# A two-layer streaming encoder step on one core: where the conditioning pieces stand in a pair chunk's weight stream, and thirteen identity products at the start

## The chip, the cores and the metric

The kernel runs on one core of one Trainium2 chip. The metric is device time in microseconds (us), the median of several runs. TensorE (PE) multiplies matrices, VectorE (DVE) and ScalarE (ACT) work on elements, SyncE (SP) issues nearly all of the DMAs, GpSimd (POOL) does little here. "Clock" is the share of full speed that TensorE was granted, as the profile records it.

## What is computed

Two groups of rows, 1024 prompt rows and 32 sample rows of width 1024, go through two layers that share their weights. Cut to what matters:

```python
for i in range(2):
    mod = silu(c) @ w_ada[i] + b_ada[i]            # c: 1 x 1024, w_ada[i]: 1024 x 6144
    sh1, sc1, gt1, sh2, sc2, gt2 = split(mod, 6)
    h = rmsnorm(x, g[i, 0]) * (1 + sc1) + sh1
    mix = sgu_mixer(h) if i == 0 else pool_mixer(h)
    x = x + gt1 * rmsnorm(mix, g[i, 1])
    h = rmsnorm(x, g[i, 2]) * (1 + sc2) + sh2
    f = square(relu(h @ ffn_w_up[i])) @ ffn_w_down[i]   # 1024 -> 4096 -> 1024
    x = x + gt2 * rmsnorm(f, g[i, 3])
```

The six vectors of `mod` are the conditioning. Their matrix `w_ada` is 24 MB a layer, and each of the two `c` is one vector, so the conditioning is mostly loading. The first mixer starts with `v = gelu(h @ w_in)[:, 2048:]`.

## The kernel before

**Tiles.** The 1056 columns (rows of the reference, turned) are three tiles: 0 and 1 with 384 prompt columns each, 2 with 256 prompt and 32 sample columns. Each float32 operand is split in a high and a low part of the type fp32r (`split`, L1325; `w_split`, L498), and a product is three matmuls: high by high, high by low, low by high (`products`, L1061).

**The weight stream.** All weights come from HBM in one fixed order, the list `stream`. An entry is a 512 KB load; SP issues the loads in the order of the list into three raw buffers (`RAW_SLOTS`, L31; `issue`, L460). `stream_step` (L723) then consumes an entry: a weight is split by ACT (high part, L542) and DVE (low part) into one of 16 tiles (`do_w`, L534), and `need_w` gives it to PE. The raw buffer goes back when its last reader is done, and the next load can start.

**Conditioning pieces.** Among the weights stand pieces of `w_ada`. A late piece is 256 rows by 512 columns (`add_wide`, L297), and DVE multiplies it with the conditioning and adds it up in four instructions on 128 x 512 (`do_ada`, L614, tile `aa`). Every fourth piece ends with two transposes and two sums, and every second such end with small matmuls on PE (`fold`, L654). `some_ada(n)` puts the next n pieces of the list `rest` into the stream.

**Pair chunks.** In the feed-forward part, the list `passes` (L384) names for each layer seven pair chunks: 512 of the 4096 hidden columns each, for tiles 0 and 1 together. `w_chunk` (L352) writes a pair chunk's entries into the stream: four up weights, j = 0 to 3, in two groups of two, kinds `one` and `two`; then four down weights, q = 0 to 3. Its argument `ada` is the number of conditioning pieces that go between them: in layer 0 it is 5 for the first pair chunk, 6 for the next five and 1 for the last; in layer 1 it is 1 or 2 while pieces are left. A group of two up weights is turned by `quads` (L503), in four steps, into sums and differences of quarter matrices, A1, S31, S24 and A22, which need seven quarter products instead of eight (`pair_item`, L1569). PE's order in `up` (L1618) is: `pfa` from A1, `pfb` from S31, `pfa` from S24, `pfb` from S24, `pfa` from S31, `pfc` from A1, `pfa` from A22. Each product has twelve matmuls. Between the uses of an accumulator ACT copies it (`copy`, L1608, its line is L1610); PE may add to the accumulator only after that copy. `up(0)` and `up(1)` are followed by `down` (L1662), whose results DVE adds into `acc`.

**What sets the order.** Python code records the work with its own count of PE and DVE time (`time`, `weave`, L815), and the framework's scheduler then sets each engine's final order; the engines run that order strictly. The start, L1169 to L1242, is ordered by hand (`tc.manual_schedule()`) and stays as written.

**The start.** x arrives and is turned by PE (`x_turn`, L688). The first pieces of `w_ada` are multiplied on PE: four column blocks at a time (`do_ada_pe`, L578), then ACT copies the sum (`adas`, L595), and `fold` (L597) transposes it on PE with the identity `ident` and lets DVE finish a quarter of the scale (`sc1`, `sl` 4 to 7) or of the shift (`sh1`, `sl` 0 to 3). `first_norm` (L1038) makes `hh` (high, ACT) and `hl` (low, DVE) for two blocks of 128 rows of x at a time, and `early_mm` (L1125, matmuls at L1138) multiplies them with the first weight of the v half into `pv`: for three column blocks, twelve matmuls with the weight's high part and then six with its low part `wl_v`. The scratch accumulators of this stretch are a ring of three PSUM tiles (`ps_ms`, L143).

Of the kernel before, what the change touches and what calls it, by code (L numbers as in the profile page):

```python
# [15 lines left out]
P = 128  # L16
# [19 lines left out]
def tile_stream_encoder_step(  # L36
# [27 lines left out]
    mm = nc.tensor.matmul  # L64
# [47 lines left out]
    ident = const.tile([P, P], F32, name="ident")  # L112
# [24 lines left out]
    def ps_up(name):  # L137
        return psum.tile([P, 512], F32, tag="pu", bufs=2, name=name)
# [4 lines left out]
    def ps_ms(name):  # L143
        return psum.tile([P, 512], F32, tag="pm", bufs=3, name=name)
# [45 lines left out]
    def load_vectors(queue, i, part):  # L190
        at = sum(k for _, k in rows[i][: part.start])
        for ap, k in rows[i][part]:
            queue.dma_start(vec_rows[i][at : at + k, :P], ap)
            at += k
# [7 lines left out]
    def bring(func):  # L202

        act(out=junk1, in_=epsT, func=func)

    def turn_conditions():
        raw = vec_rows[2]
        act(out=raw[0:16, P : 2 * P], in_=raw[0:16, :P], func=AF.Silu)
        pt = ps_ms("csilT")
        nc.tensor.transpose(pt[:, 0:16], raw[0:16, P : 2 * P], ident[0:16, 0:16])  # L210
        nc.vector.tensor_copy(csil, pt[:, 0:16].rearrange("p (v k) -> p k v", v=NV))
        nc.vector.tensor_copy(csil32[:, :, 0:NV], csil)

    def turn_vectors():
        for raw, v in zip(vec_rows, vecs):
            n = v.shape[1]
            pt = ps_ms("rowT")
            nc.tensor.transpose(pt[:, :n], raw[:n, :P], ident[:n, :n])
            nc.vector.tensor_copy(v, pt[:, :n])
# [22 lines left out]
    def add_w(key, ap, shape, kind="w"):  # L242
        stream.append((kind, key, ap, shape))
# [108 lines left out]
    def w_chunk(n, ada=0):  # L352
        l, c, tiles, m = passes[n]
        left = [ada]

        def one_ada():
            if left[0] > 0:
                left[0] -= 1
                some_ada(1)

        for j in range(4 * m):
            f = 4 * c + j
            add_w(
                ("up", n, j),
                ffn_w_up[l][:, f * P : (f + 1) * P].rearrange("(k p) f -> p k f", p=P),
                (8, P),
                ("one", "two")[j % 2] if tiles == PAIR else "w",
            )
            if j % 2 == 1:
                one_ada()  # L370
        w = 256 // m
        for q in range(4 * m):
            add_w(
                ("dn", n, q),
                ffn_w_down[l][c * 512 : (c + m) * 512, q * w : (q + 1) * w].rearrange(
                    "(j p) d -> p j d", p=P
                ),
                (4 * m, w),
            )
            one_ada()  # L380

    every = list(range(NT))
    PAIR = every[:2]
# [10 lines left out]
    def some_ada(n):  # L394
        for _ in range(min(n, len(rest))):
            add, l, j = rest.pop(0)
            add(l, j)
# [62 lines left out]
    def issue():  # L460
        while state["issued"] < len(stream):
            k = state["issued"]
            kind, key, ap, shape = stream[k]
            if in_raw(k):
                if state["raw"] == RAW_SLOTS:
                    return
                state["raw"] += 1
                r = t_raw(f"raw{k}")
            elif kind == "x":
                r = x_rows[min(key // 3, NT - 1)]  # L470
                r = r[:, key % 3] if key < 6 else r
            else:
                r = w_tile(f"raw{k}")
            if kind == "x" and key < 6:
                i = nc.sync.dma_start(r, ap.rearrange("t (k n) -> t k n", n=P))
            elif kind == "x":
                for j in range(ap.shape[0] // 32):
                    for a in range(4):
                        i = nc.sync.dma_start(
                            r[32 * a : 32 * a + 32, 4 * (key - 6) + j],  # L480
                            ap[32 * j : 32 * j + 32].rearrange("s (k a m) -> s a k m", a=4, m=32)[:, a],
                        )
            else:
                i = nc.sync.dma_start(r.rearrange("p (a b) -> p a b", a=shape[0]), ap)
            raws[k] = r
            loads[key] = i.ins
            state["issued"] += 1
# [191 lines left out]
    def run_deferred(force=False):  # L679
        n = len(deferred)  # L680
        while n > 0 and (force or deferred[0][0] <= time["pe"]):
            deferred.pop(0)[1]()
            n -= 1
# [39 lines left out]
    def stream_step():  # L723

        if not subs and stream[state["next"]][0] == "one":
            issue()
            state["next"] += 1
        k = state["next"]
        kind, key, ap, shape = stream[k]
        issue()  # L730
        run_deferred()
        if kind == "two":
            if not subs:
                quads(key[1], key[2], raws.pop(k - 1), raws.pop(k))
            subs.popleft()[1]()
            if not subs:
                state["next"] += 1
            issue()
            return
        r = raws.pop(k)  # L740
        if kind == "w":
            do_w(key, r)
        elif kind == "wide":
            do_ada(*key, r, 512)
        elif kind == "ada":
            if k < first_ada:
                do_ada_pe(*key, r)
            else:
                do_ada(*key, r, 256)
        else:  # L750
            do_x(key, r)
        state["next"] += 1
        if in_raw(k):
            state["raw"] -= 1
        issue()
# [352 lines left out]
    def statistics(h):  # L1108
        while next(h) != "statistics":
            pass  # L1110

    def stream_to(kind, key):
        k = max(i for i, s in enumerate(stream) if s[0] == kind and s[1] == key)
        while state["next"] <= k:
            stream_step()
        run_deferred()
# [38 lines left out]
    def fold():  # L1155
        pe_folds.pop(0)()

    def turn():
        x_turns.popleft()()

    def lo():
        late_lo.popleft()()

    def row(h):

        next(h)
        next(h)

    with tc.manual_schedule():  # L1169
        load_vectors(nc.scalar, 2, slice(0, 2))  # L1170
        issue()
        load_vectors(nc.gpsimd, 0, slice(0, 1))
        load_vectors(nc.gpsimd, 1, slice(0, 1))
        load_vectors(nc.gpsimd, 2, slice(2, 4))
        bring(AF.Silu)
        stream_to("x", 0)
        turn_conditions()
        stream_to("x", 2)
        bring(AF.Sqrt)
        next(h0)  # L1180
        next(h0)
        stream_to("ada", (0, 4, 0))
        turn_vectors()
        stream_to("ada", (0, 4, 1))
        next(h0)
        statistics(h0)
        fold()
        next(h0)
        stream_to("ada", (0, 0, 1))
        fold()  # L1190
        stream_to("w", ("v", 0, 0))
        next(h0)
        late_hi.pop()()
        next(h0)
        lo()
        early_mm((0, 1, 2), 0)
        stream_to("x", 5)
        next(h1)
        turn()
        next(h1)  # L1200
        stream_to("ada", (0, 5, 1))
        turn()
        fold()
        next(h1)
        statistics(h1)
        turn()
        early_ps.extend(ps_up(f"pv0_{b}") for b in (3, 4))
        next(h1)
        row(h1)
        stream_to("ada", (0, 1, 1))  # L1210
        next(h0)
        early_mm((3,), 0)
        fold()
        early_mm((4,), 0)
        for q in range(1, 4):
            stream_to("w", ("v", 0, q))
            row(h0)
            lo()
            next(h1)
            row(h1)  # L1220
            if q == 3:
                stream_to("w", ("v", 1, 0))
            early_mm((0, 1), q)
            if q < 3:
                conditions(q + 1)
                fold()
                next(h0)
            early_mm((2,), q)
            if q < 3:
                fold()  # L1230
            early_mm((3, 4), q)
        bring(AF.Gelu_apprx_tanh)
        ps = ps_ms("pv0_5")
        v_mm(ps, 0, 5, range(KB))
        early_end((0,))
        stream_to("w", ("v", 1, 1))
        early_end((1, 2))
        stream_to("w", ("v", 1, 2))
        early_end((3,))
        stream_to("w", ("v", 1, 3))  # L1240
        early_end((4,))
        v_end(ps, 0, 5)  # L1242
# [40 lines left out]
    for p, b in v_order:  # L1283
        ps = ps_dn(f"pv{p}_{b}")
# [882 lines left out]
```

## Time and profile before

| | |
|---|---|
| median of 3 runs | 2106.61 us (2105.29 to 2107.28) |
| the profiled execution's own time | 2106.9 us |
| its span, first to last instruction | 2105.1 us |
| mean granted clock | 0.998 |
| POOL busy | 22.3 us |
| HBM read, written | 262.18 MB, 30.66 MB |
| mean HBM traffic over the span | 139 GB/s |

The profile is one execution. The 1.8 us between its time and its span lie before the first and after the last instruction. A group of instructions is named by its line, its engine and the tiles that it writes and reads, out<-in. A helper's line stands for all of its calls: L80 is every DVE operation of the kernel's own wrappers, and L1066 to L1068 are the three matmuls of a product. A busy PE is not a PE at its peak, since matmuls overlap, so the starts of matmuls in a row are read instead. PE loads weights on a path of its own (PEld, 96% busy).

### The profile page before, as it was taken

The numbers are of one execution on the slowest core, as the hardware profiler recorded it, in microseconds if no ns is written. First come the engines' busy times: TensorE is split into PE (matmuls) and PEld (weight loads), VectorE is DVE, ScalarE is ACT, GpSimd is POOL, SyncE is SP. The second block draws the span as 40 slices with busy tenths as digits, with TensorE's granted clock in tenths as the row PEclk, the third lists the DMA queues.
The fourth block names the chain that finished last, engine by engine and source line by source line (L and its number), as shares of the span: only waits on it lengthen the run. The fifth ranks groups of instructions, "written<-read, shape, count | busy, mean of one in ns | idle before, by whom it ended". The sixth has DMA issues, their size and how long they took to land.

```text
span 2105.1 us, 32717 instructions
## 1 busy us (share of the span) xinstructions
PE 2084.7 (99%) x12786; PEld 2013.1 (96%) x12786; DVE 1569.3 (75%) x2811; ACT 1034.3 (49%) x1853; POOL 22.3 (1%) x44
## 2 busy tenths in 40 slices
PE   8999999999999999999999999999999999999998
PEld 6878999999999999999999999999999999999998
DVE  6788737556869988888767989897868654579554
ACT  5634322234447644344446766776435443365555
POOL 0000000000000000000000000000000000001100
PEclk9999999999999999999999999999999999999999
DMA  8586524243524443443334667643223221148862
GB/s 295 159 268 213 187 79 135 85 150 106 159 70 156 130 126 113 128 126 115 114 96 130 207 198 238 192 140 106 92 76 109 88 80 52 54 125 233 202 180 93
DMA packets 397040, 294.98 MB, mean 140 GB/s; under 512 B 46638, under 2 KB 360278, under 8 KB 396884
## 3 DMA queue, kind: packets, MB, share of 16 engines
q1 hardware_dynamic: 395956, 291.60, 45.8%
q8 instruction: 100, 1.64, 0.3%
q0 software_dynamic: 896, 1.28, 0.2%
q14 instruction: 56, 0.46, 0.1%
q10 hardware_dynamic: 32, 0.01, 0.0%
HBM read 262.18 MB, written 30.66 MB: 139 GB/s over the span
## 4 chain that ended last, share of the span: by engine, by line
PE 89%; DVE 6%; ACT 2%; DMA 2%; issue 1%; SPq 0%; DVEq 0%; ACTq 0%
PE pg L1067 11%; PE pg L1066 11%; PE pg L1068 11%; PE pf L1066 4%; PE pf L1068 4%; PE pf L1067 4%; PE po L1066 3%; PE po L1067 3%; PE po L1068 3%; PE pfa L1604 3%; PE pfa L1606 3%; PE pfa L1605 3%; PE pu L1066 3%; PE pu L1068 3%; PE pu L1067 3%; PE pv L1092 2%
## 5 line engine op out<-in xcount | busy, mean ns | idle before, releaser
L1066 PE MATMUL pg<-fh,wh_dn 128*128 128x384 f32 (+1 forms) x960 | 311.2, 325 | 0.1
L1067 PE MATMUL pg<-fl,wh_dn 128*128 128x384 f32 (+1 forms) x960 | 310.8, 324 | 0.0
L1068 PE MATMUL pg<-fh,wl_dn 128*128 128x384 f32 (+1 forms) x960 | 310.0, 323 | 0.0
L80 DVE TENSOR_TENSOR acc<-acc,pg 128x384 f32<-128x384 f32 (+1 forms) x272 | 144.7, 533 | 111.9 <-PE pg L1068 110.7
L80 DVE TENSOR_TENSOR wl_dn<-raw,wh_dn 128x1024 fp32r<-128x1024 f32 x136 | 166.2, 1223 | 70.0 <-ACT wh_dn L542 36.7
L80 DVE SCALAR_TENSOR_TENSOR aa<-raw,csil,aa 128x512 f32<-128x512 f32 (+1 forms) x364 | 207.9, 621 | 13.0 <-DMA raw<-in_w_ada_dram 12.9
L1066 PE MATMUL pf<-hh,wh_up 128*128 128x288 f32 (+1 forms) x640 | 195.4, 305 | 0.4 <-ACT wh_up L542 0.4
L1067 PE MATMUL pf<-hl,wh_up 128*128 128x288 f32 (+1 forms) x640 | 194.0, 303 | 0.0
L1068 PE MATMUL pf<-hh,wl_up 128*128 128x288 f32 (+1 forms) x640 | 193.7, 303 | 0.0
L542 ACT ACTIVATE wh_dn<-raw 128x1024 fp32r<-128x1024 f32 x136 | 143.8, 1057 | 88.7 <-PE pf L1067 33.8
L1066 PEld LDWEIGHTS pg<-fh,wh_dn 128*128 128x128 f32 x960 | 180.2, 188 | 1.4 <-ACT fh L1326 1.0
L1067 PEld LDWEIGHTS pg<-fl,wh_dn 128*128 128x128 f32 x960 | 180.3, 188 | 0.9 <-DVE fl L80 0.4
L1068 PEld LDWEIGHTS pg<-fh,wl_dn 128*128 128x128 f32 x960 | 180.2, 188 | 0.0
L542 ACT ACTIVATE wh_up<-raw 128x1024 fp32r<-128x1024 f32 x80 | 84.7, 1059 | 80.3 <-PE pg L1067 44.9
L1066 PEld LDWEIGHTS pf<-hh,wh_up 128*128 128x128 f32 x640 | 120.1, 188 | 1.1 <-ACT wh_up L542 0.7
L80 DVE TENSOR_TENSOR wl_up<-raw,wh_up 128x1024 fp32r<-128x1024 f32 x80 | 97.6, 1221 | 31.0 <-ACT wh_up L542 30.5
L1068 PEld LDWEIGHTS pf<-hh,wl_up 128*128 128x128 f32 x640 | 120.5, 188 | 0.3 <-DVE wl_up L80 0.3
L1067 PEld LDWEIGHTS pf<-hl,wh_up 128*128 128x128 f32 x640 | 120.2, 188 | 0.4
L80 DVE TENSOR_TENSOR wl_up_S<-raw,wh_up_S 128x512 fp32r<-128x512 f32 (+1 forms) x84 | 71.9, 866 | 55.8 <-PE pfb L1605 51.5
L1066 PE MATMUL pg<-fx,wh_dn 128*128 128x288 f32 (+1 forms) x352 | 109.4, 311 | 0.4 <-ACT fx L1326 0.4
L1067 PE MATMUL pg<-fx,wh_dn 128*128 128x288 f32 (+1 forms) x352 | 108.3, 308 | 0.0
L1068 PE MATMUL pg<-fx,wl_dn 128*128 128x288 f32 (+1 forms) x352 | 108.2, 307 | 0.0
(400 smaller groups left out, 5549.5 us busy)
## 6 DMA issues: line engine op xcount, KB each, us to landing
raw<-in_ffn_w_up_dram SPq DMA_DIRECT2D x136, 512.0 KB, 4.1
raw<-in_ffn_w_down_dram SPq DMA_DIRECT2D x136, 512.0 KB, 3.9
raw<-in_w_ada_dram SPq DMA_DIRECT2D x90, 512.0 KB, 4.3
raw<-in_sgu_w_in_dram SPq DMA_DIRECT2D x40, 512.0 KB, 4.0
xd<-acc SPq DMA_DIRECT2D x8, 1536.0 KB, 8.3
raw<-in_sgu_w_out_dram SPq DMA_DIRECT2D x24, 512.0 KB, 3.8
xo_r<-xd SPq DMA_DIRECT2D x32, 384.0 KB, 4.1
vd<-vt SPq DMA_DIRECT2D x32, 256.0 KB, 3.6
```

The costliest lines, as they stand in the source:

```text
L80: return op(out, *args, **kw)
L542: act(out=wh, in_=r, func=AF.Copy)
L1066: mm(ps[:, :n], wh, rh, start=i == 0, stop=False)
L1067: mm(ps[:, :n], wh, rl, start=False, stop=False)
L1068: mm(ps[:, :n], wl, rh, start=False, stop=i == last)
L1092: mm(ps[:m, :], a_h, wh[:, o : o + 512], start=k == 0, stop=False)
L1604: mm(ps[:, :n], wh[:, o], rh, start=first and k == 0, stop=False, skip_group_check=True)
L1605: mm(ps[:, :n], wh[:, o], rl, start=False, stop=False, skip_group_check=True)
L1606: mm(ps[:, :n], wl[:, o], rh, start=False, stop=k == HK - 1, skip_group_check=True)
```

## The change

Two edits. In the stream, the conditioning piece that stood behind the second up weight of a chunk (and the one behind the fourth) becomes a single one behind the fourth, and a second piece is allowed behind the last down weight. With six pieces the order was u0 u1 A u2 u3 A d0 A d1 A d2 A d3 A, and becomes u0 u1 u2 u3 A d0 A d1 A d2 A d3 A A. With five it was u0 u1 A u2 u3 A d0 A d1 A d2 A d3, and becomes u0 u1 u2 u3 A d0 A d1 A d2 A d3 A. The number of pieces is the same. In the start, four products of the identity with itself stand ahead of the fold that ends the first quarter of `sh1` (the second fold in the program), and nine behind it. They write to a scratch accumulator that nobody reads.

```diff
--- before.py
+++ after.py
@@ -366,7 +366,7 @@ w_chunk
                 ("one", "two")[j % 2] if tiles == PAIR else "w",
             )
-            if j % 2 == 1:
+            if j == 4 * m - 1:
                 one_ada()
@@ -378,6 +378,8 @@ w_chunk
             one_ada()
+            if q == 4 * m - 1:
+                one_ada()
@@ -1161,6 +1163,12 @@
+    def keep_clock(n):
+
+        ps = ps_ms("idle")
+        for _ in range(n):
+            mm(ps[:, :P], ident, ident, start=True, stop=True)
+
@@ -1187,7 +1195,9 @@
         stream_to("ada", (0, 0, 1))
+        keep_clock(4)
         fold()
+        keep_clock(9)
         stream_to("w", ("v", 0, 0))
```

## The prediction, made before the changed kernel was run

> **What bounds the kernel now.** I read the page's busy times first. Engine, busy us, share of the span:
>
> ```profile
> PE 2084.7 (99%) x12786; PEld 2013.1 (96%) x12786; DVE 1569.3 (75%) x2811; ACT 1034.3 (49%) x1853; POOL 22.3 (1%) x44
> ```
>
> TensorE is the bound and is nearly never idle: 2105.1 - 2084.7 leaves 20.4 us. An edit that leaves PE's work alone can only win from those 20.4 us, or from time in which PE runs slowly. So I asked next who PE waits for (us in total, times, longest):
>
> ```profile
> PE pv L1138 <- ACT hh L1026: 1.8, 2, 1.1
> PE pfb L1604 <- ACT b L1610: 1.5, 4, 0.5
> PE pfa L1604 <- ACT a L1610: 1.4, 2, 0.7
> ```
>
> The first row is the start, the other two are the pair chunks: 2.9 us in six waits. That is all that the edit of the stream can remove. Then I cut the start in stretches of 1 us (columns: length, busy us of PE, PEld, DVE, ACT and POOL, granted clock, DMA share, GB/s), and looked at one long stretch behind it:
>
> ```profile
> 16.00:17.00 1.00, 0.00 (x0) 0.00 (x0) 0.31 (x2) 0.62 (x2) 0.00 (x0) 1.00 1.03 389
> 17.00:18.00 1.00, 0.96 (x2) 0.49 (x3) 0.62 (x1) 1.00 (x3) 0.00 (x0) 0.60 1.01 362
> 18.00:19.00 1.00, 1.00 (x3) 0.81 (x3) 0.95 (x2) 1.00 (x3) 0.00 (x0) 0.50 1.09 387
> 19.00:20.00 1.00, 1.00 (x4) 0.71 (x4) 0.80 (x1) 0.97 (x2) 0.00 (x0) 0.50 1.09 385
> 20.00:21.00 1.00, 1.00 (x5) 0.82 (x4) 0.00 (x0) 0.97 (x3) 0.00 (x0) 0.69 1.09 387
> ```
>
> ```profile
> 41.00:697.00 656.00, 655.12 (x3859) 614.62 (x3858) 477.35 (x992) 276.22 (x487) 2.49 (x8) 1.00 0.47 145
> ```
>
> The clock column shows what busy time hides. From 17.2 to 20.6 us PE runs at half clock: (1 - 0.60)/0.5 + 1 + 1 + (1 - 0.69)/0.5 = 3.4 us, right behind a microsecond in which PE did nothing. Behind 41 us PE is dense (655.12 of 656), so what the start wins or loses reaches the end nearly whole.
>
> **The start, part by part.** PE in order of time (start, duration, line, tiles, count, idle before):
>
> ```profile
> 13.86 1.07 PE L583 MATMUL ada<-raw,csil 128*32 128x256 f32 x16
> 15.49 0.44 PE L600 MATMUL adat<-ident,adas 128*128 128x128 f32 x2 [0.56 <-ACT adas L595]
> 17.04 0.68 PE L1138 MATMUL pv<-wh_v,hh 128*128 128x512 f32 x1 [1.11 <-ACT hh L1026]
> 17.70 0.80 PE L1138 MATMUL pv<-wh_v,hl 128*128 128x512 f32 x1
> 18.29 0.63 PE L1138 MATMUL pv<-wh_v,hh 128*128 128x512 f32 x1
> 18.72 0.63 PE L1138 MATMUL pv<-wh_v,hl 128*128 128x512 f32 x1
> ...
> 20.75 0.39 PE L1138 MATMUL pv<-wh_v,hh 128*128 128x512 f32 x1
> 20.98 0.40 PE L1138 MATMUL pv<-wh_v,hl 128*128 128x512 f32 x1
> 21.67 1.52 PE L1138 MATMUL pv<-wl_v,hh 128*128 128x512 f32 x6
> 23.03 1.03 PE L695 MATMUL xT<-ident,x_rows 128*128 128x128 f32 x8
> ```
>
> The gaps are 0.56 us ahead of the fold and 1.11 us behind it. At half clock a v product follows the one before after 18.72 - 18.29 = 0.43 us, at full clock after 20.98 - 20.75 = 0.23.
>
> An identity product does not exist before. The nearest row is the other plain float32 product of 128 x 128:
>
> ```profile
> 26.17 0.83 PE L850 MATMUL pb_h<-r_h,ones 128*128 128x128 f32 x6
> L850 PE MATMUL pb_h<-r_h,ones x12: 275/275/377, 12.8 to 26.7; 128*128 128x128 f32 x12
> ```
>
> Three such products leave six records, so a record follows the last after (0.83 - 0.275)/5 = 0.11 us, and a product costs 0.22 at full clock. From below, a transpose has one record (the eight of the last PE row, 0.11 each); from above, half clock doubles it. I take 0.22: the same operation and shape. Four take 0.9 us in a gap of 0.56, nine take 2.0 in one of 1.11. So they overfill both gaps, and what matters is what arrives late. The first four begin at 14.77 (a follower starts some 0.16 before the last matmul's end: 21.67 + 1.52 - 23.03) and are done at 15.66, so the fold starts 0.17 us late, and with it the shift, `hh` and `hl`. These rows give DVE and then ACT behind the fold:
>
> ```profile
> 17.02 0.62 DVE L80 SCALAR_TENSOR_TENSOR hl<-mt,mod,hh 128x384 fp32r<-128x384 f32 x1 [0.68 <-ACT hh L1026]
> 18.05 0.62 DVE L80 SCALAR_TENSOR_TENSOR hl<-mt,mod,hh 128x384 fp32r<-128x384 f32 x1 [0.41 <-ACT hh L1026]
> 18.59 1.22 DVE L80 TENSOR_TENSOR wl_v<-raw,wh_v 128x1024 fp32r<-128x1024 f32 x1
> ```
>
> ```profile
> 16.38 0.61 ACT L1026 ACTIVATE hh<-mt,mod 128x384 fp32r<-128x384 f32 x1 [0.41 <-DVE mod L80]
> 16.90 0.61 ACT L540 ACTIVATE wh_v<-raw 128x512 fp32r<-128x512 f32 x1
> 17.42 0.60 ACT L1026 ACTIVATE hh<-mt,mod 128x384 fp32r<-128x384 f32 x1
> ```
>
> With 0.17 added, the first `hl` is there at 17.81, the second at 18.84, `wl_v` at 19.98. The fold's two transposes take 0.22, so PE ends the nine at 15.66 + 0.22 + 2.0 = 17.9, and all that it then needs is ready in time. At full clock the twelve products with the high part take 12 x 0.23, to 20.6, and the six with the low part run to 22.0. Before, the turn of x behind them began at 23.03. **The start wins 1.0 us.** The bounds: 1.6 if the products cost nothing (the second `hl` at 18.67, then 6 + 6 products, is 21.4); a loss of 0.6 is worked out in a rival. Behind the products only PE's own work is queued.
>
> Whether the clock holds is the choice here. Both gaps, 1.67 us, lie in the 3.4 us ahead of the halving. A later stretch, with 0.61 us idle, keeps the clock:
>
> ```profile
> 29.00:30.00 1.00, 0.39 (x1) 0.19 (x1) 0.85 (x2) 1.00 (x3) 0.00 (x0) 1.00 1.10 401
> ```
>
> So I take it that a half idle stretch halves the clock and a filled one doesn't. [...]
>
> **The stream, part by part.** No work is added: the pieces are as many as before, each four DVE instructions of 0.73 us:
>
> ```profile
> L80 DVE SCALAR_TENSOR_TENSOR aa<-raw,csil,aa x364: 443/734/753, 72.3 to 1574.6; 128x512 f32<-128x512 f32 x98, 128x256 f32<-128x256 f32 x84
> ```
>
> One piece of 2.9 us leaves the middle of the two up groups and one comes behind the last down weight. On SP one 512 KB load moves past two up weights or more; nothing moves on POOL, and PE's quarter folds move by some products. What could be late next are the next chunk's up weights, behind 2.9 us more of DVE work:
>
> ```profile
> 927.88 1.23 DVE L80 TENSOR_TENSOR wl_up_A<-raw,wh_up_A 128x1024 fp32r<-128x1024 f32 x1
> ```
>
> ```profile
> 950.97 0.34 PE L1604 MATMUL pfa<-hh,wh_up_A 128*128 128x384 f32 x1
> ```
>
> That split ends 22 us before PE uses it, so 2.9 cost nothing. What are the six waits then? Three of them (SP, ACT and PE of the first; PE alone of the other two):
>
> ```profile
> 901.97 0.37 SPq L484 DMA_DIRECT2D raw<-in_w_ada_dram  x1
> 903.04 0.37 SPq L484 DMA_DIRECT2D raw<-in_ffn_w_down_dram  x1
> ```
>
> ```profile
> 907.75 1.06 ACT L542 ACTIVATE wh_dn<-raw 128x1024 fp32r<-128x1024 f32 x1 [1.54 <-DMA raw<-in_ffn_w_down_dram]
> ```
>
> ```profile
> 909.24 0.44 PE L1604 MATMUL pfb<-hh,wh_up_S 128*128 128x384 f32 x1 [0.32 <-ACT b L1610]
> 784.00 0.44 PE L1604 MATMUL pfa<-combo_R,wh_up_S 128*128 128x384 f32 x1 [0.70 <-ACT a L1610]
> 1521.70 0.44 PE L1604 MATMUL pfa<-combo_R,wh_up_S 128*128 128x384 f32 x1 [0.68 <-ACT a L1610]
> ```
>
> They are not caused by the piece between the groups. ACT stands at the split of the second down weight, whose load could only be issued at 903.04, and the accumulator's copy waits behind it in ACT's order. The issue waits for a raw buffer of the second up group, whose last split waits for PE to free weight tiles. The new instruction order has the same neighbours there: piece, down weight, piece, down weight on SP, and on ACT in the chunks behind the second the split still ahead of the copy. So I leave the four `pfb` waits at 1.5 us. In the second chunk (784.00) ACT now makes the S24 split two instructions earlier, and the down weight's load follows; I take half of 0.70, 0.35. At 1521.70 the order is a new one: `pfc` no longer precedes, and the copies stand behind more of the pooling mixer's ACT work. That can remove 0.68 or double it; I take half off, 0.35. **Together 0.7 us**, between 2.9 (all waits) and a loss of 1.4 (the two `pfa` waits doubled).
>
> **Sum.** Against the profiled execution's own 2106.9 us: 2106.9 - 1.0 - 0.7 = **2105.2 us**. The execution lies 0.3 above the median of 2106.61, so this is 1.4 below the median, inside the 2 us over which the three runs spread (2105.29 to 2107.28).
>
> **Rivals.**
> - The clock halves all the same. The nine have 0.7 us left at 17.2 and take 1.4, to 18.6; 4.7 v products follow at 0.43 to 20.6, and 13.3 at 0.23 end at 23.6: 0.6 later than before. 2106.9 + 0.6 - 0.7 = 2106.8. [...] Chance 0.17.
> - The stream's edit does not reach the waits at all, since the raw buffers set them: only the start wins, 2105.9. For it: the four rows left alone above. Chance 0.23.
> - Slower: in each of the five chunks with six pieces the second down weight's load falls behind one more piece. Two loads issued at 901.97 and 903.04 are both there at 907.75, one alone takes
>
> ```profile
> raw<-in_w_ada_dram SPq DMA_DIRECT2D x90, 512.0 KB, 4.3
> ```
>
>  so one more costs 907.75 - 901.97 - 4.3 = 1.5 us on ACT, which already makes PE wait: 5 x 1.5 = 7.5, 2106.9 + 7.5 = 2114. It decides from 0.9 us per chunk. Against it: SP's order puts two pieces side by side only behind the last down weight. Chance 0.06.
> - All six waits go and the start wins its bound: 2106.9 - 2.9 - 1.6 = 2102.4, with the restarts of PE behind the waits 0.2% faster. Chance 0.04.
>
> **How the numbers follow.** The forecast has 0.50, and with the first two rivals 0.90 lies within 0.2% (4.2 us, about what a measurement of this kernel can tell from no change). Slower has 0.06, faster 0.04. The range runs from 2103.0 (start 1.6, stream 2.3 of its 2.9) to 2108.0 (start a loss of 0.6, stream one of 0.5), and leaves out the last two rivals.
>
> **What would show it.** PE from 14.9 to 18 without a gap, clock 1.00 from 17 to 21, the turn of x at about 22.0; the `pfb` waits still four with about 1.5 us; the split of the next chunk's first up weight some 3 us later and never waited for. I am wrong if the clock column still holds 0.50 behind the products, or if PE's waits for ACT copies change by more than 1.5 us.

## The result, and the profile after

The changed kernel took **2112.94 us** (median of 9 runs, 2110.28 to 2116.49) against 2106.61 us for the kernel before on the same chip: ratio 1.003, 95% interval 1.002 to 1.004. It is slower by 6.3 us where 1.4 us faster had been forecast, and outside the range of 2103 to 2108. The profiled execution is the median one.

The page's busy times of the changed kernel:

```profile
PE 2085.9 (99%) x12812; PEld 2015.2 (95%) x12812; DVE 1570.5 (74%) x2811; ACT 1033.2 (49%) x1853; POOL 22.3 (1%) x44
```

PE is busy 1.2 us more, with 26 matmuls more; nothing else was added. The other 5 us are time in which PE is idle. PE's waits (us in total, times, longest):

```profile
PE pfb L1614 <- ACT b L1620: 4.4, 5, 1.5
...
PE psp L1430 <- DVE aa L80: 1.8, 1, 1.8
PE pfa L1614 <- ACT a L1620: 1.2, 3, 0.5
PE ada L660 <- DVE part L646: 1.0, 1, 1.0
...
PE pv L1140 <- ACT hh L1028: 0.7, 1, 0.7
PE pg L1069 <- DVE fx L80: 0.7, 1, 0.7
PE pg L1069 <- DVE combo_R L80: 0.7, 1, 0.7
```

Lines are shifted: L1614 is before's L1604, L1430 its L1420, L1028 its L1026. The `pfb` row went from 1.5 to 4.4 us, `psp` from 0.6 to 1.8, and `pv`, the start, from 1.8 to 0.7. Rows for `part`, `combo_R` and DVE's `fx` are new: there PE waits for DVE, at tiles that are not weights.

Where along the span is it lost? I took the start of the same matmul in both traces and the difference, after less before, at the borders of the stretches:

| where (us in the trace of before) | after less before, us |
|---|---|
| 231.8, first `psp` | -0.6 |
| 250.7, second gate's `psp` | +0.6 |
| 681.2, first pair chunk of layer 0 begins | +0.5 |
| 759.5, second pair chunk | +3.5 |
| 824.4, third pair chunk | +4.1 |
| 1077.9, last pair chunk of layer 0 | +4.6 |
| 1344.0, tile 2's part of layer 0 nearly done | +6.3 |
| 1540.4, layer 1's pair chunk with two pieces begins | +4.7 |
| 1637.7, the chunk behind it | +6.3 |
| 2097.7, PE's end | +6.4 |

So there are five places: 250 us (1.2 lost), the first two pair chunks (3.6), 1220 to 1290 us (1.7), one chunk of layer 1 (1.6), and a gain of 1.6 between 1344 and 1540. These are one execution of each kernel, so a few tenths at a place can be chance.

**The start did what it should.** PE of the changed kernel (start, duration, line, tiles, count), then the granted clock in stretches of 1 us:

```profile
15.08 1.16 PE L1170 MATMUL idle<-ident 128*128 128x128 f32 x8
16.08 0.38 PE L602 MATMUL adat<-ident,adas 128*128 128x128 f32 x2
16.29 2.17 PE L1170 MATMUL idle<-ident 128*128 128x128 f32 x18
...
22.42 1.03 PE L697 MATMUL xT<-ident,x_rows 128*128 128x128 f32 x8
```

```profile
17.00:18.00 1.00, 1.00 (x12) 1.00 (x11) 0.45 (x1) 1.00 (x3) 0.00 (x0) 1.00 1.00 394
18.00:19.00 1.00, 1.00 (x8) 0.88 (x7) 0.59 (x2) 1.00 (x3) 0.00 (x0) 1.00 1.07 383
19.00:20.00 1.00, 1.00 (x6) 0.83 (x5) 1.00 (x2) 0.97 (x3) 0.00 (x0) 1.00 1.11 387
```

There is no gap, the clock holds at 1.00, and the turn of x begins at 22.42 instead of 23.03. A product costs (18.22 - 16.29) / 9 = 0.21 us (18.22 is the first `pv`), close to the 0.22 taken. But the win is gone at 250 us. The gate's `psp` in the changed kernel:

```profile
251.21 1.47 PE L1430 MATMUL psp<-wr,vl 128*128 128x128 f32 x11 [1.76 <-DVE aa L80]
```

and in the kernel before:

```profile
250.65 1.58 PE L1420 MATMUL psp<-wr,vl 128*128 128x128 f32 x12 [0.57 <-DVE aa L80]
```

The view names DVE's `aa`, which `psp` does not read. What `psp` reads is `vl`, a part of v that is reloaded from DRAM. SP's issues of this load, before and after:

```profile
247.66 0.38 SPq L1374 DMA_DIRECT2D vl<-vd  x1
248.18 0.38 SPq L1384 DMA_DIRECT2D vl<-vd  x1
```

It lands 2.9 us later in both, at 250.52 and 251.07. In every one of the 18 profiles `psp` starts 0.13 or 0.14 us behind this landing, whatever engine the view names, so it is the reload that PE waits for. SP issues it when a store of `vst` ahead of it has landed (SP waits 1.3 us for that), and DVE makes `vst` between its conditioning pieces: at 244.74 before, at 245.22 in the changed kernel. This chain does not start at PE. PE comes 0.6 us earlier, the load 0.5 us later, and PE waits longer. How much of an early start passes this point differs between the profiles: nothing here, 0.1 of 1.3 us in products_only (below), 0.5 of 1.5 in best_few, 1.2 of 1.5 in only_p2.

**The first two pair chunks.** DVE of the changed kernel, the operations that waited for the load of a piece between 690 and 795 us:

```profile
702.43 0.48 DVE L80 TENSOR_SCALAR aa<-raw,csil 128x512 f32<-128x512 f32 x1 [1.62 <-DMA raw<-in_w_ada_dram]
718.43 0.75 DVE L80 SCALAR_TENSOR_TENSOR aa<-raw,csil,aa 128x512 f32<-128x512 f32 x1 [0.64 <-DMA raw<-in_w_ada_dram]
761.77 0.75 DVE L80 SCALAR_TENSOR_TENSOR aa<-raw,csil,aa 128x512 f32<-128x512 f32 x1 [2.46 <-DMA raw<-in_w_ada_dram]
787.45 1.42 DVE L80 SCALAR_TENSOR_TENSOR aa<-raw,csil,aa 128x512 f32<-128x512 f32 x2 [1.39 <-DMA raw<-in_w_ada_dram]
```

and of the kernel before, in the same stretch:

```profile
759.78 2.08 DVE L80 SCALAR_TENSOR_TENSOR aa<-raw,csil,aa 128x512 f32<-128x512 f32 x3 [1.59 <-DMA raw<-in_w_ada_dram]
```

So it is DVE that stands for pieces: 6.1 us instead of 1.6. The two up groups now follow each other through the three raw buffers, so the piece behind them is loaded only when DVE already wants it, and DVE's order holds the sums for S31, the low parts and `combo_R` behind it. How the first of these waits reaches PE (ACT, then PE, of the changed kernel):

```profile
703.56 0.63 ACT L519 ACTIVATE wh_up_S<-raw 128x512 fp32r<-128x512 f32 x1 [3.30 <-DVE raw L80]
704.09 0.47 ACT L1620 ACTIVATE b<-pfb 128x384 f32<-128x384 f32 x1
```

```profile
704.62 0.44 PE L1614 MATMUL pfb<-hh,wh_up_S 128*128 128x384 f32 x1 [0.74 <-ACT b L1620]
```

ACT's split of S31 waits for DVE's sum, and the copy of `pfb` stands behind that split. In the two chunks PE waits 3.6 us in all, against 0.9 before; about 2.7 of it ends on DVE in this way or directly (`combo_R` 0.69, `part` 1.00). DVE has little time to make up for it. The two chunks in the kernel before:

```profile
697.00:761.00 64.00, 64.00 (x370) 63.79 (x369) 59.86 (x107) 31.53 (x55) 0.00 (x0) 1.00 0.51 156
761.00:824.00 63.00, 62.07 (x361) 61.01 (x360) 57.01 (x102) 26.81 (x48) 0.00 (x0) 1.00 0.39 117
```

DVE (the third busy time) was busy 59.86 of 64 and 57.01 of 63 us: 94% and 90%, against 75% over the span.

**The chunk of layer 1.** Its last two pieces stood ahead of the first down weight; now one stands behind it, ahead of the second. ACT of the changed kernel:

```profile
1596.57 0.47 ACT L1620 ACTIVATE a<-pfa 128x384 f32<-128x384 f32 x1
1599.77 1.06 ACT L544 ACTIVATE wh_dn<-raw 128x1024 fp32r<-128x1024 f32 x1 [2.73 <-DMA raw<-in_ffn_w_down_dram]
1600.73 0.47 ACT L1620 ACTIVATE b<-pfb 128x384 f32<-128x384 f32 x1
```

The copy of `pfb` stands behind a split that stands for its load, and PE waits 1.50 us for the copy. This is the mechanism of the prediction's slower rival with its price of 1.5 us, in one chunk where the rival had put it in five. The first pair chunk has it too, for 0.50 us: at 722.04 PE waits for a copy of `pfa` behind a split that stood 2.03 us for its load.

### The profile page after: what moved, and what is told of

Its sections match the earlier page's. It is cut to its first block, busy times and chain, and to the rows that moved or that the text cites. A ratio compares the mean times of both kernels' runs of the same rounds, so it can differ in the third digit from the quotient of the medians.

```text
span 2111.1 us, 32783 instructions
## 1 busy us (share of the span) xinstructions
PE 2085.9 (99%) x12812; PEld 2015.2 (95%) x12812; DVE 1570.5 (74%) x2811; ACT 1033.2 (49%) x1853; POOL 22.3 (1%) x44
## 4 chain that ended last, share of the span: by engine, by line
PE 90%; DVE 4%; DMA 3%; ACT 2%; issue 1%; DVEq 0%; ACTq 0%
PE pg L1069 11%; PE pg L1068 11%; PE pg L1070 11%; PE pf L1068 4%; PE pf L1070 4%; PE pf L1069 4%; PE po L1068 3%; PE po L1069 3%; PE po L1070 3%; PE pfa L1614 3%; PE pfa L1616 3%; PE pfa L1615 3%; PE pu L1068 3%; PE pu L1070 3%; PE pu L1069 3%; PE pv L1094 2%
```

## The experiments

All ratios are to runs of the kernel before on the same chip, made together with the kernel (its medians: 2106.78 for products_only, stream_only, only_p2 and only_p17; 2108.01 for only_p3to7 and the three `tiny` kernels; 2107.71 for best, best_few, few4 and p2_late; 2108.24 for the other four), with 95% intervals. "Drift" is the growth of the difference to before from 616 us (the first feed-forward matmul) to PE's end, from the profiles, which leaves the start and the wait at 250 us out. A drift is one execution against one, and chance is in it: only_p17, which changes nothing ahead of layer 1, falls 0.6 us behind before between 824 and 1078 us.

### Which half loses

```diff
 products_only: the kernel before +  keep_clock(4); fold(); keep_clock(9)
 stream_only:   the changed kernel - keep_clock(4), - keep_clock(9)
 only_p2, only_p17, only_p3to7: the kernel before with the new order in some chunks alone
-            if j % 2 == 1:
+            if j == 4 * m - 1 or j == 1 and not (n == 2):
...
+            if q == 4 * m - 1 and (n == 2):
+                one_ada()
```

`n` is the index in `passes`: 2 to 8 are the pair chunks of layer 0, 15 to 21 those of layer 1, and 17 is the one with two pieces.

products_only:

> The thirteen identity products alone, the stream as before. Theory: the clock holds and the turn of x comes 0.6 us earlier, but at 249.7 us PE waits for DVE, which stands there on the schedule of its loads and not on PE's, so the win is gone by then: the time is within 0.7 us of before (2106.6, from 2105.9 to 2107.3), and the wait of psp for aa grows from 0.6 us to 1.2 or more. Rival A, the prediction's: the win reaches the end, 0.6 to 1.0 us faster (2105.6 to 2106.0). Rival B: the products cause the loss (they shift every load behind them): 3 us slower or more.

stream_only:

> The edit of the stream alone, without the identity products. Theory: all of the loss is here; the chunks of layer 0, the stretch behind them and layer 1 lose the 5.8 us that they lost in the profile of the changed kernel: 2112.4, between 2111 and 2114. Rival B: the products cause the loss, then this is within 1 us of before.

only_p2:

> Of the stream's edit only the first pair chunk (u0 u1 u2 u3 A d0 A d1 A d2 A d3 A, five pieces), all else as before. Theory: this chunk has a loss of its own, 2.9 us in the profile of the changed kernel, since DVE then stands 1.6 us for the load of the piece that now comes right behind both groups, with the sums for S31 behind it: 2109.5, between 2108.5 and 2110.5. Rival C: no single chunk matters, any change of the stream shifts all that follows by several us: then the loss lies behind the chunk and not in it. Rival D: the loss in this chunk came from where the chunk began (0.5 us late), not from its order: within 0.7 us of before.

only_p17:

> Of the stream's edit only layer 1's third pair chunk, the one with the last two pieces (u0 u1 A u2 u3 A d0 d1 d2 d3 becomes u0 u1 u2 u3 A d0 A d1 d2 d3), all else as before. Theory: the second down weight's load now stands behind a piece, its split on ACT comes later, and the copy that PE's pfb needs waits behind it: one pfb wait of 1.5 us in this chunk that before did not have, 2108.1, between 2107.3 and 2108.9. Rival: the wait is cancelled by what the chunk wins where no piece stands between the groups: within 0.5 us of before.

only_p3to7:

> Of the stream's edit only the five pair chunks of layer 0 with six pieces (u0 u1 u2 u3 A d0 A d1 A d2 A d3 A A), all else as before. Theory: they hold what stream_only loses and only_p2 and only_p17 don't (3.6 - 1.5 - 0.7 = 1.4 us), most of it in the first of them, where PE's fold waits 1.0 us for DVE's sum at 792 us and the 784 us wait stays: 2108.2, between 2107.3 and 2109.2. Rival: the parts are not additive and this one alone loses 2.5 us or more.

| kernel | median, us | ratio |
|---|---|---|
| products_only | 2109.95 | 1.0016 (1.0008 to 1.0025) |
| stream_only | 2110.39 | 1.0018 (1.0009 to 1.0027) |
| only_p2 | 2108.26 | 1.0004 (0.9996 to 1.0013) |
| only_p17 | 2107.49 | 1.0004 (0.9996 to 1.0013) |
| only_p3to7 | 2105.30 | 0.9986 (0.9977 to 0.9995) |

By the medians the halves lose 3.2 and 3.6 us, 6.8 in all, near the 6.3. My theory, that the products cost nothing and all is in the stream, fell. So did the idea that the stream's parts add up: 1.5 + 0.7 - 2.7 is -0.5 by the medians, and the whole edit loses 3.6. Of the parts, the losses of only_p2 (under the range expected) and only_p17 are not clear of noise. In the five chunks with six pieces, where a loss was expected, the new order by itself is a gain clear of noise.

products_only was expected to wait at 250 us for DVE. It waits 1.8 us, but for the reload of v, as said above.

Also seen here: stream_only, only_p2 and only_p3to7 have no products, and in their profiled executions the clock did not halve at 17 us. Of the ten profiles taken without products at the second fold, before included, seven kept the clock, with the same gaps of 0.56 and 1.11 us; at 231.8 us these seven are 0.7 to 1.5 us ahead of before without any product at the fold. The halving that the prediction read from one profile is a matter of the execution, and so is what can be won by preventing it.

### Why the stream's parts don't add up

```diff
 best:      the new order in passes 3 to 8, 15 and 16
 best_p2:   best and pass 2 (all but 17)
 best_p17:  best and pass 17 (all but 2)
 p2_late:   the kernel before, pass 2 as u0 u1 u2 u3 d0 A d1 A d2 A d3 A A
```

best:

> The stream's edit in all pair chunks but the first of layer 0 and the one of layer 1 with two pieces (those two as before); no products. Theory: the first one's loss comes from its own order and passes on to the next, and the last one's from the piece between its first two down weights, so without them the gain of only_p3to7 stays and the wait at 1522 us may halve: 2.5 to 3.5 us faster than before (2103.5 to 2104.5 by a before of 2107). Rival (the gain of only_p3to7 is a lucky set of late loads): within 1 us of before.

best_p2:

> best with the edit in the first pair chunk too (all chunks but the one with the last two pieces). Theory: a piece that the first chunk passes on takes DVE time in the second, which is 90% busy, so the second chunk loses its gain: 3 to 4 us over best, 0.5 to 2 us slower than before. Rival (parts add up): 1.5 us over best, 0.5 to 1 us faster than before.

best_p17:

> best with the edit in the chunk with the last two pieces too (all chunks but the first). Theory: one pfb wait more near 1595 us, 0.7 to 1.5 us over best: 0.8 to 1.6 us faster than before. Rival (the whole edit's loss is here): 3 us slower than before or more.

p2_late:

> The stream of before, but in the first pair chunk the first piece stands behind the first down weight: u0 u1 u2 u3 d0 A d1 A d2 A d3 A A (in only_p2 it is u0 u1 u2 u3 A d0 A d1 A d2 A d3 A). Theory: only_p2 loses in this chunk since DVE stands for the piece's load ahead of the sums for S31; here no piece is between those, so the wait of pfb near 703 us stays away, and the chunk loses under 0.7 us; what is pushed into the next chunk can cost there. Rival (DVE, 94% busy in this chunk before, simply has too little time once a piece moves backward): the chunk and the next one lose 1.5 us or more together.

| kernel | median, us | ratio |
|---|---|---|
| best | 2105.42 | 0.9991 (0.9982 to 1.0000) |
| best_p2 | 2110.68 | 1.0012 (1.0003 to 1.0021) |
| best_p17 | 2107.32 | 0.9996 (0.9987 to 1.0004) |
| p2_late | 2107.89 | 0.9999 (0.9990 to 1.0008) |

only_p3to7 beats both kernels clear of noise; best does so with an interval that just reaches 1, and by less than expected (1.9 us by its ratio instead of 2.5 to 3.5). The first chunk added to best costs 0.0021 of 2108 us, 4.4 us, though it cost 0.9 (1.5 by the medians) alone; the chunk with two pieces adds 1 us, near what it cost alone. So what doesn't add up is the first chunk and the second: in new order both, DVE stands for pieces' loads in a row. The totals of DVE's waits for `raw<-in_w_ada_dram` between 690 and 795 us, one line from each kernel's waits: only_p2,

```profile
DVE aa L80 <- DMA raw<-in_w_ada_dram: 2.0, 4, 0.7
```

best,

```profile
DVE aa L80 <- DMA raw<-in_w_ada_dram: 2.9, 4, 1.6
```

and best_p2:

```profile
DVE aa L80 <- DMA raw<-in_w_ada_dram: 6.2, 4, 2.7
```

Either order alone leaves 2 to 3 us, which DVE can take up; both give 6.2, as in the changed kernel (6.1) and in stream_only (5.9). In best_p2's profile the two chunks lose 2.0 and 1.3 us against before; in best's the first loses 0.9 and the second wins 1.0. Over all profiles, the three kernels with both chunks in new order lose 3.1 to 3.6 us in the two, and every other kernel comes out between 0.6 us faster and 0.5 slower there. p2_late, without the piece right behind the groups, is level with before, as expected, and its two chunks together lose nothing in the profile. Why the other chunks gain is not shown in full.

### Why the products lose

In products_only no instruction of another engine changes place, but for two neighbouring memsets of DVE at the very start; only the 13 products are new. Yet its drift is 2.4 us. One thing does move: PE's instructions. They come by DMA too. The page of the kernel before:

```profile
q8 instruction: 100, 1.64, 0.3%
```

100 packets of 16 KB for 2 x 12786 matmuls and weight loads are 256 instructions a packet, and tiny64 (below), with 256 instructions more, has 101. These packets have a queue of their own, q8, and not the weights' queues that an expectation below names. Thirteen products are 52 instructions, a fifth of a packet, and in products_only most packets come 2.5 to 6 us earlier than before against the same work (4.5 in the middle). So the next kernels changed how many instructions stand ahead, and where.

```diff
 in place of keep_clock, behind the second fold (tiny13, tiny32, tiny64; n products):
+            mm(ps[:, :8], ident, ident[:, :8], start=True, stop=True)
 one ahead of the second fold, three behind it (few4):
+            mm(ps[:, :384], ident, A(0, 0), start=True, stop=True)
 best_few: best and few4's products
 in gate(), at its second call (fp26: 26 of them, no products at the start):
+                    mm(x[:, :8], onesr, onesr[:, :8], start=True, stop=True)
 in gate(), at its second call (products_fill: products_only and two of these):
+                    mm(x[:, :384], ident, A(0, 0), start=True, stop=True)
```

tiny13:

> The kernel before with thirteen identity products of 8 columns (in place of 128) behind the second fold, where PE waits 1.11 us anyway; nothing else, all orders as before. They add 26 matmuls and 26 weight loads, as the changed kernel's thirteen do. Theory (PE's instructions arrive in 100 packets of 16 KB, 256 instructions each, on the queues that also carry the weights; 52 more instructions move each such packet to another moment, and a load that PE needs soon is then late by up to 1 us): the loss of products_only is here too, though the products take next to no time of PE: 2109 to 2111, with extra waits behind 700 us and none at the start. Rival (the loss comes from the start being 1.2 us early, or from PE time that the products take): within 0.7 us of before.

tiny32:

> As tiny13, with 32 such products: 128 instructions, half a packet of PE's instructions. Theory: another phase of the packets, so another set of late loads: the drift behind 250 us differs from that of before and of tiny13, with a sign that the theory doesn't give (between -1 and +4 us); the start costs at most 32 times 0.22, less the 1.1 us of the gap. Rival (time of PE alone counts): the drift behind 250 us is zero and the total only rises by what the start costs.

tiny64:

> As tiny13, with 64 such products: 256 instructions, exactly one packet of PE's instructions, so that every later packet is asked for at the same place of the program as before. Theory: the start costs more (at most 64 times 0.22 us less the gap of 1.1, likely 3 to 8 us), but behind 250 us the waits are those of before: a drift of less than 0.5 us from there to the end in the profile. Rival (more instructions are worse in themselves): the drift is that of tiny13 or more.

few4:

> The kernel before with the same PE time of products at the second fold as in the changed kernel, but in four long ones instead of thirteen (identity by 384 columns of x, one ahead of the fold, three behind it): 8 matmuls and 8 weight loads, 16 instructions instead of 52. Stream as before, all orders as before. Theory of the instruction packets: the packets move by a sixteenth of their distance (1 us) instead of 4.3 us, so most of the 3.2 us that products_only loses is not lost: within 1.2 us of before, and the drift behind 250 us under 1 us. Rival (filled gaps, PE time or the earlier start cost the 3.2 us, however many instructions they are): 2 us slower or more, as products_only.

best_few:

> best with the four long products of few4. Theory: the start is not the bound behind 250 us, where PE waits for DVE in any case, so what the held clock wins (0 to 1.2 us, by execution) is gone there: within 0.7 us of best. Rival (the prediction's): 0.6 to 1.0 us faster than best. Rival: products cost 3 us here too.

fp26:

> The kernel before with 26 small products of fp32r ones (8 columns) in the up products of the mixer some 8 us ahead of the wait at 250 us: 26 matmuls and 26 weight loads, 52 instructions as in the changed kernel, nothing else, all orders as before. The start is that of before; the direct cost is at most 26 times 0.11 us, of which the wait at 250 us takes up 0.6. Theory of the instruction packets: drift of 2 to 3 us behind 250 us, 2109 to 2112 in all by a before of 2107. Rival (early arrival at 250 us): no drift, 0 to 2 us of direct cost.

products_fill:

> products_only with two long products (identity by 384 columns of x, 1.3 us) some 8 us ahead of the wait at 250 us, so that PE comes there as late as before. Theory of the instruction packets: nothing changes for them (60 instructions in place of 52), 2.5 to 3.5 us slower than before. Rival (early arrival): the wait at 250 us is 0.5 us, the clock holds there, and the time is within 1 us of before.

| kernel | instructions added | median, us | ratio | drift in the profile, us |
|---|---|---|---|---|
| products_only | 52 | 2109.95 | 1.0016 (1.0008 to 1.0025) | 2.4 |
| products_fill | 60 | 2111.41 | 1.0017 (1.0008 to 1.0026) | 3.5 |
| fp26 | 52 | 2113.60 | 1.0028 (1.0017 to 1.0040) | 5.3 |
| tiny13 | 52 | 2117.64 | 1.0043 (1.0030 to 1.0056) | 6.0 |
| few4 | 16 | 2109.87 | 1.0008 (0.9999 to 1.0017) | 3.3 |
| tiny32 | 128 | 2120.90 | 1.0059 (1.0046 to 1.0073) | 3.1 |
| tiny64 | 256 | 2133.22 | 1.0118 (1.0104 to 1.0132) | 2.1 |
| best_few | 16 | 2106.60 | 0.9992 (0.9984 to 1.0001) | -0.7 |

products_fill (in which eleven of PE's matmuls near 255 us change places as well) rules the rival out that PE's early arrival at 250 us costs the time: its wait there is 0.8 us, the clock held there, and it is slower by 0.0017, 3.6 us, about what the packets' theory had. fp26 leaves the start alone and loses more. The packets show best near 1222 us, where DVE adds `xo_r`, reloaded from DRAM, and PE's next `fx` depends on what follows in DVE's order. DVE in the kernel before:

```profile
1217.82 0.96 DVE L80 TENSOR_TENSOR acc<-acc,xo_r 128x768 f32<-128x768 f32 x1 [0.23 <-DMA xo_r<-xd]
1219.06 0.95 DVE L80 TENSOR_TENSOR acc<-acc,xo_r 128x768 f32<-128x768 f32 x1
```

in fp26:

```profile
1221.83 0.96 DVE L80 TENSOR_TENSOR acc<-acc,xo_r 128x768 f32<-128x768 f32 x1 [1.94 <-DMA xo_r<-xd]
1223.07 0.95 DVE L80 TENSOR_TENSOR acc<-acc,xo_r 128x768 f32<-128x768 f32 x1
```

and PE of fp26 behind it:

```profile
1226.36 0.40 PE L1066 MATMUL pg<-fx,wh_dn 128*128 128x288 f32 x1 [1.96 <-ACT fx L1326]
```

The DMA queues while the `xo_r` loads are on their way, in the kernel before (1214.8 to 1218.8 us):

```profile
q1 hardware_dynamic: 1145, 1.34, 96.9%
```

and in fp26 (1216 to 1222 us):

```profile
q1 hardware_dynamic: 2298, 1.92, 96.8%
q8 instruction: 1, 0.02, 0.9%
```

q1, which carries the weights and this load, keeps the 16 DMA engines 97% busy, and in fp26 a packet of PE's instructions falls into this stretch. Over all 18 profiles, with the place taken as 1218.4 us in before (the middle of its two additions) and carried over by PE's matmuls: in the five kernels with 52 or 60 instructions more (the changed one among them) a packet comes 1.2 to 2.0 us ahead of this place, the second `xo_r` load takes 4.9 to 5.5 us, and PE waits 0.8 to 2.0 us. In the twelve others without tiny32 no packet comes between 9 and 1 us ahead; the load takes 3.6 to 4.2 us and PE waits 0.0 to 0.65. tiny32 doesn't fit: its packet comes 8.9 us ahead, before the load is issued, and yet the load takes 4.75 us and PE waits 1.3. So a packet is not all that can make this load late. Some 63 us on, the same five wait 0.2 to 0.8 us where none of the twelve waits at all. tiny64, with one whole packet more, has its packets back at before's places (1.5 us behind the first place, where before has 1.7) and nearly before's waits: 0.6 and 0.0 us against 0.4 and 0.0.

A third place, near 1545 us, is the clearest: there PE needs `wg`, a matrix of the pooling mixer. In products_only, fp26 and tiny13, and in no other profile, a packet comes 0.8 to 1.0 us behind the issue of its load. The load takes 3.6, 4.2 and 3.8 us there, against 2.5 to 2.8 in the other fifteen, and PE waits 0.9, 1.5 and 1.1 us for it. PE of fp26:

```profile
1552.18 0.51 PE L1985 MATMUL pp<-acc,wg 128*128 128x288 f32 x1 [1.52 <-DMA wg<-in_pool_w_grp_dram]
```

Over all weight loads behind 260 us in the eight profiles with before's stream: a load with a packet in its first 2.5 us takes 4.61 us on the mean (198 loads), one without 4.25 (1944). With a packet 1 to 4 us before its issue, or 5 to 8 behind, it is 4.27 on both sides. The loads are the same in all eight, so each can be compared with itself: 108 loads have a packet in some profiles and none in others, and take 0.35 us longer with it on the mean. So a packet goes with 0.35 us more for a load, and with more than 1 us at the places above. How a packet would make a load longer is not shown: no run here shows the DMA engines singly.

Four expectations were missed. few4, with 16 instructions, should have drifted by under 1 us; its profile, the slowest of its eleven runs, drifts by 3.3, and its ratio can't tell 0 from 3.6 us. tiny64 should have drifted by under 0.5; it was 2.1. At the three places of the packets both behave nearly as before, so the rest of their drift is elsewhere, among others in `pfb` waits of 2.3 and 2.4 us against 1.5. tiny13 (2109 to 2111 expected) and fp26 (a drift of 2 to 3) lose more than the packets were to cost.

What part of the loss the packets explain is seen at the three places only. PE waits there 2.1 us in products_only, against 0.4 in before: 1.7 us of its drift of 2.4. It is 2.0 us in products_fill, 3.6 in tiny13 and 4.3 in fp26, and 1.7 at the first two places in the changed kernel. In tiny13 and products_fill some 1.6 us more are lost between 1220 and 1290 us than the longer waits take: there the clock halved right behind the first wait. The remainder stays open: that small changes of time move loads that are just in time is my guess, and I could not tie each of the other waits to a packet.

best_few shows that few4's products add nothing to best that can be seen (0.9992 against 0.9991). best's profile held the clock without them, so this does not price a halved clock.

## Why the prediction was wrong, step by step

The miss is mostly two prices that the sum put at nothing. The stream's edit was to win 0.7 us and loses 3.6 alone, since DVE's time was not in the sum; the products were to win 1.0 and lose 3.2 alone, since nothing beyond the start was in it. The lost win of the start is the smaller part.

- **"What the start wins or loses reaches the end nearly whole."** This step failed. In the changed kernel's profile the clock holds and 0.6 us are won up to 232 us (1.0 forecast, which compared the products with an execution in which the clock had halved). The busy share behind 41 us (655.12 of 656) was right and said nothing: the 0.57 us wait of `psp` at 250 us was in before's trace, and there PE meets a load, `vl`, whose time PE does not set.
- **"So they overfill both gaps, and what matters is what arrives late."** Right on PE, 0.21 us a product; but the price was not PE's time. Thirteen products were a cost beyond the start that no term of the sum had.
- **"That split ends 22 us before PE uses it, so 2.9 cost nothing."** This step failed too. It is true of that split, which still ends 18 us ahead, and says nothing of the rest of DVE's work. DVE stood for the piece itself, and what PE waited for was `combo_R`, `part` and the copies behind DVE's order. The chunk windows would have shown DVE 94% and 90% busy; I read only its 75% over the span.
- **"So I leave the four `pfb` waits at 1.5 us", "I take half of 0.70", "half off".** In the changed kernel's profile there are five, 4.4 us: one in the first pair chunk (0.7), three in layer 0 (2.2) and the new one in layer 1 (1.5). The wait at 784.00 is gone, but two of 0.38 and 0.31 us for copies of `pfa` have come in the same chunk, so nothing of the 0.70 is won. The one at 1521.70 is gone. In all, the waits for these copies went from 2.9 to 5.6 us, more than the 1.5 that the prediction named as a sign of being wrong.
- **The slower rival (2114, chance 0.06).** Its time is 1 us from the median, by another sum, which is luck. Its mechanism cost 1.5 us in one chunk of layer 1 and 0.50 in the first pair chunk; in the five chunks that it named, the `pfb` waits only went from 1.5 to 2.2 us; "SP's order puts two pieces side by side only behind the last down weight" missed that the layer 1 chunk with two pieces now has one between its first two down weights, where it had none.
- **"The stream edit does not reach the waits at all."** Wrong for the five chunks with six pieces: there alone the edit wins 2.7 us by the medians. In that kernel's profile the waits for the two copies fall from 2.9 to 2.1 us, near the 0.7 forecast; the rest of the gain is not traced.

## What to carry to other kernels

Read the busy share of every engine in the very stretch that an edit touches: here DVE, 94% and 90% busy before, stood 6.1 us for loads that came a little late in the changed kernel, and PE waited some 2.7 us for what was queued behind it. A win at the start counts only as far as the next wait for something that the winner does not pace: here the 0.6 us won up to 232 us were gone at 250 us, where PE waited 1.76 us for the reload of v. When a view names as the releaser something that the instruction does not read, compare the landing of what it does read. Instructions added to fill a gap of PE come by DMA too: here 256 more of them (tiny64) were one packet more, 101 instead of 100, and a load with a packet in its first 2.5 us took 0.35 us more on the mean.

## What the runs showed of the hardware

- In tiny64 matmuls of 8 columns without a gap did not bring the clock back. PE is busy throughout on such products up to 42.15 us, and the granted clock (the column behind the five busy times) is half from 17.6 to 44.9 us:

```profile
27.00:42.00 15.00, 15.00 (x72) 15.00 (x72) 0.00 (x0) 0.00 (x0) 0.00 (x0) 0.50 0.77 278
```

- In this stretch at half clock a record of these 8 columns follows the last after 15.00 / 72 = 0.21 us, and in few4 at half clock one of 128 columns (`psp`) did so too. The weight loads (PEld, the second busy time above) are as busy as PE; that they set this time is my guess, and no run tells. The 128 records in tiny64, the first of them at full clock:

```profile
16.24 26.05 PE L1168 MATMUL idle<-ident 128*128 128x8 f32 x128
```

- In three profiles the clock was half for 3.4 us right behind a wait in the middle of dense work: in few4 at 251.0 us behind 1.9 us, in tiny13 and products_fill near 1225 us behind 1.96 and 1.81 us. In the changed kernel, products_only and fp26 waits as long (1.76, 1.80 and 1.96 us) passed without it. Where it halved near 1225 us, some 1.6 us were lost beyond the wait.
